# Uneven row groups (65 and 63 rows per partition) in a top-2 dispatch kernel, and one early store less

## The chip, the cores and the metric

The kernel runs on one core of a Trainium2 chip. The metric is the device time of one execution in microseconds; lower is better. The other cores are idle.

## The reference

```python
batch, seq, hidden, n_experts, k = 16, 1024, 512, 8, 2
logits_max = np.max(router_logits, axis=-1, keepdims=True)
probs = np.exp(router_logits - logits_max)
probs = probs / np.sum(probs, axis=-1, keepdims=True)
topk_indices = np.argsort(probs, axis=-1)[..., -k:]
topk_probs = np.take_along_axis(probs, topk_indices, axis=-1)
topk_probs = topk_probs / np.sum(topk_probs, axis=-1, keepdims=True)
x_expanded = x[:, :, np.newaxis, :].repeat(k, axis=2)
return (x_expanded * topk_probs[..., np.newaxis]).astype(np.float32)
```

There are 16384 rows (tokens) of 512 float32 values. For each row, the softmax weights of the two best of eight experts are normalized to a sum of one, the smaller first. The output holds each row of x twice, once times each weight. So 33.6 MB of x and 0.5 MB of logits are read, and 67.1 MB are written: an x row has 2 KiB, an output row (both copies) 4 KiB.

## The kernel before

Row p x 128 + m lies on partition p: each of the 128 partitions owns 128 consecutive rows, m = 0 to 127. In memory two neighbouring partitions therefore stand 128 rows apart, 256 KiB in x and 512 KiB in the output.

`top2_weights` finds the two largest of eight logits by a tree of maxima and minima on VectorE (lines 26 to 36), takes their difference (L39), and makes both weights as sigmoids of it on ScalarE (L41, L42). The result `WA` holds two weights for every row.

The 128 rows of a partition are worked off in two groups of 64. `xs` is a buffer for 64 rows of x on every partition, and `osp` one for 16 rows of output. A group consists of

- the loads into `xs` (L101): 16 rows each in group 0; 2, 2, 4, 8 and then three times 16 rows in group 1 (`LOADS`);
- one multiplication on VectorE for each tile of rows (L105), which writes both products of each row, and a store of that tile (L113).

There is no room for 64 rows of output beside `xs`, so most tiles write their output over rows of `xs` that are done with. The plan of a group: rows 0 to 15 go to `osp`; rows 16 to 31 over rows 0 to 31 of `xs` (`low`); rows 32 to 39 and 40 to 47 to the two halves of `osp`, once the store of rows 0 to 15 has landed; rows 48 to 63 in tiles of 8, 4 and 4 over rows 32 to 63 (`high`).

In group 0 the first tile is split. Two rows are multiplied and stored first, and that store is issued by ScalarE's queue; the other 14 rows follow. Every other transfer is issued by SyncE's queue, in the order of the program: all loads of a group stand before its stores, and the loads of group 1 behind the last store of group 0. A load or a multiplication that overwrites rows waits until the store that reads them has landed; a queue works in order, so what stands behind a waiting instruction waits too.

Of the kernel before, what the change touches and what calls it, by code (L numbers as in the profile page):

```python
# [1 line left out]

# [4 lines left out]

F32 = mybir.dt.float32
ALU = mybir.AluOpType
ACTF = mybir.ActivationFunctionType  # L10
P = 128


def top2_weights(nc, pool, logits, M, E):

    hi, lo, n = None, None, E
    while n > 1:  # L20
        n //= 2
        if hi is None:
            a, b = logits[:, :, 0:n], logits[:, :, n : 2 * n]
            nhi = pool.tile([P, M, n], F32, tag=f"hi{n}")
            nlo = pool.tile([P, M, n], F32, tag=f"lo{n}")
            nc.vector.tensor_tensor(nhi, a, b, op=ALU.max)  # L26
            nc.vector.tensor_tensor(nlo, a, b, op=ALU.min)  # L27
        else:
            a, b = hi[:, :, 0:n], hi[:, :, n : 2 * n]
            nhi = pool.tile([P, M, n], F32, tag=f"hi{n}")  # L30
            nlo = pool.tile([P, M, n], F32, tag=f"lo{n}")
            tmp = pool.tile([P, M, n], F32, tag=f"tmp{n}")
            nc.vector.tensor_tensor(tmp, lo[:, :, 0:n], lo[:, :, n : 2 * n], op=ALU.max)  # L33
            nc.vector.tensor_tensor(nlo, a, b, op=ALU.min)  # L34
            nc.vector.tensor_tensor(nlo, nlo, tmp, op=ALU.max)  # L35
            nc.vector.tensor_tensor(nhi, a, b, op=ALU.max)  # L36
        hi, lo = nhi, nlo
    dlt = pool.tile([P, M], F32, tag="dlt")
    nc.vector.tensor_tensor(dlt, hi[:, :, 0], lo[:, :, 0], op=ALU.subtract)  # L39
    WA = pool.tile([P, M, 2], F32, tag="WA")  # L40
    nc.scalar.activation(WA[:, :, 0], dlt, ACTF.Sigmoid, scale=-1.0)  # L41
    nc.scalar.activation(WA[:, :, 1], dlt, ACTF.Sigmoid, scale=1.0)  # L42
    return WA

LOADS = [[16] * 4, [2, 2, 4, 8] + [16] * 3]


@with_exitstack  # L50
def kernel(
    ctx: ExitStack,
    tc: tile.TileContext,
    x: bass.AP,
    router_logits: bass.AP,
    k: bass.AP,
    out: bass.AP,
):
    nc = tc.nc
    B, S, D = x.shape  # L60
    E = router_logits.shape[-1]
    N = B * S
    assert int(k) == 2 and E == 8 and N % P == 0
    M = N // P

    GROUP = 64
    L = 16
    x_v = x.rearrange("b s d -> (b s) d").rearrange("(p m) d -> p m d", p=P)
    o_v = out.rearrange("b s k d -> (b s) k d").rearrange("(p m) k d -> p m k d", p=P)
    rl_v = router_logits.rearrange("b s e -> (b s) e").rearrange(  # L70
        "(p m) e -> p m e", p=P
    )

    wpool = ctx.enter_context(tc.tile_pool(name="wpool", bufs=1))
    logits = wpool.tile([P, M, E], F32)
    nc.sync.dma_start(logits, rl_v)  # L76
    WA = top2_weights(nc, wpool, logits, M, E)

    xs = wpool.tile([P, GROUP, D], F32)
    osp = wpool.tile([P, L, 2, D], F32)  # L80


    low = xs[:, : 2 * L, :].rearrange("p (r k) d -> p r k d", k=2)
    high = xs[:, 2 * L :, :].rearrange("p (r k) d -> p r k d", k=2)
    h = L // 2
    e = 2
    begin = [[(0, e, osp[:, :e]), (e, L - e, osp[:, e:])], [(0, L, osp)]]
    plan = [
        (L, L, low),
        (2 * L, h, osp[:, :h]),  # L90
        (2 * L + h, h, osp[:, h:]),
        (3 * L, h, high[:, :h]),
        (3 * L + h, h // 2, high[:, h : h + h // 2]),
        (3 * L + h + h // 2, h // 2, high[:, h + h // 2 :]),
    ]

    for g in range(M // GROUP):
        m0 = g * GROUP
        r = 0
        for n in LOADS[g]:  # L100
            nc.sync.dma_start(xs[:, r : r + n, :], x_v[:, m0 + r : m0 + r + n, :])  # L101
            r += n
        for r, n, og in begin[g] + plan:
            rows = slice(m0 + r, m0 + r + n)
            nc.vector.tensor_tensor(  # L105
                og,
                xs[:, r : r + n, :].unsqueeze(2).to_broadcast([P, n, 2, D]),
                WA[:, rows, :].unsqueeze(3).to_broadcast([P, n, 2, D]),
                op=ALU.mult,
            )  # L110

            queue = nc.scalar if rows.start == 0 else nc.sync
            queue.dma_start(o_v[:, rows], og)  # L113


# [1 line left out]
_INS = ['x', 'router_logits', 'k']  # L117
_OUTS = [((16, 1024, 2, 512), 'float32')]

_NUMBERS = {'k': 2}  # L120


# [26 lines left out]
```

## Time and profile before

| | |
|---|---|
| median of 3 runs | 241.12 us (240.81 to 241.35) |
| profiled execution | 240.86 us, span 239.1 us |
| VectorE busy | 142.4 us (60%) |
| ScalarE busy | 1.8 us |
| moved by DMA | 101.19 MB, mean 423 GB/s |
| one 16-row tile on VectorE | about 17.2 us |
| one 8-row tile on VectorE | about 8.7 us |
| loads of 16 rows | 4096 KB each, median 38.0 us from issue to landing |

The span is from the first to the last instruction of the profiled execution. A DMA share of 1.00 means that all 16 DMA engines of the core were busy all the time. A transfer's time from issue to landing includes the time in which it stands behind other transfers in its queue, so it says little about how fast the transfer itself is. The chain of work that ended last is put down to DMA for 44% and to VectorE for 36%; where a transfer is followed back to its issue, that chain names the instruction that released the issue, even when the queue was still full at that moment.

### The profile page before, as it was taken

What the parts mean: (1) busy time and instruction counts of PE and PEld (TensorE: products, weight loads), DVE (VectorE), ACT (ScalarE), POOL (GpSimd) and SP (SyncE); (2) the same over time, 40 slices, a digit from 0 to 9 for tenths busy, and PEclk for the clock granted to TensorE, in tenths of its full rate; (3) what the DMA queues carried; (4) which work ended last, traced back from release to release, by engine and by line L of the source; (5) the groups of instructions that cost most, each with busy time, mean ns of one, the idle gap of its engine ahead of it and who ended that gap; (6) DMA issues with size and microseconds to landing.
All of it is one profiled execution on the core that took longest, in us unless ns stands there. A gap on an engine that the chain in (4) does not pass through costs nothing.

```text
span 239.1 us, 121 instructions
## 1 busy us (share of the span) xinstructions
DVE 142.4 (60%) x26; ACT 1.8 (1%) x3; POOL 0.2 (0%) x4
## 2 busy tenths in 40 slices
DVE  3369999910499999400000999997008999990000
ACT  2000000000000000000000000000000000000000
POOL 0000000000000000000000000000000000000000
DMA  8999999979989899999999999999999998999996
GB/s 329 400 422 384 461 433 428 511 326 451 504 351 526 351 439 439 439 439 395 436 384 452 439 439 439 433 444 471 406 450 428 406 471 362 428 439 439 439 414 288
DMA packets 3888, 101.19 MB, mean 423 GB/s; under 512 B 432, under 2 KB 432, under 8 KB 816
## 3 DMA queue, kind: packets, MB, share of 16 engines
q1 hardware_dynamic: 3744, 100.14, 97.8%
q10 hardware_dynamic: 144, 1.05, 1.0%
HBM read 34.08 MB, written 67.11 MB: 423 GB/s over the span
## 4 chain that ended last, share of the span: by engine, by line
DMA 44%; DVE 36%; issue 7%; SPq 2%; DVEq 0%
DMA out_dram<-osp 26%; DVE osp L105 22%; DMA xs<-in_x_dram 18%; DVE xs L105 15%; SPq L101 1%; SPq L76 0%; SPq L113 0%; DVEq L105 0%
## 5 line engine op out<-in xcount | busy, mean ns | idle before, releaser
L105 DVE TENSOR_TENSOR osp<-xs,WA 128x8192 f32<-128x8192 f32 (+3 forms) x7 | 69.1, 9908 | 68.3 <-DMA xs<-in_x_dram 39.4
L105 DVE TENSOR_TENSOR xs<-xs,WA 128x4096 f32<-128x4096 f32 (+2 forms) x8 | 69.5, 8691 | 0.3
L26 DVE TENSOR_TENSOR nhi<-logits 128x512 f32<-128x512 f32 x1 | 0.7, 693 | 4.1 <-DMA logits<-in_router_logits_dram 4.1
L41 ACT ACT_TABLE_LOAD x1 | 1.3, 1283 | 0.7 <-PEq L130 0.7
L34 DVE TENSOR_TENSOR nlo<-nhi 128x256 f32<-128x256 f32 (+1 forms) x2 | 0.7, 352 | 0.0
L36 DVE TENSOR_TENSOR nhi<-nhi 128x256 f32<-128x256 f32 (+1 forms) x2 | 0.7, 352 | 0.0
L33 DVE TENSOR_TENSOR tmp<-nlo 128x256 f32<-128x256 f32 (+1 forms) x2 | 0.7, 351 | 0.0
L35 DVE TENSOR_TENSOR nlo<-nlo,tmp 128x256 f32<-128x256 f32 (+1 forms) x2 | 0.7, 350 | 0.0
L27 DVE TENSOR_TENSOR nlo<-logits 128x512 f32<-128x512 f32 x1 | 0.7, 686 | 0.0
L41 ACT ACTIVATE WA<-dlt 128x128 f32<-128x128 f32 x1 | 0.3, 316 | 5.9 <-DVE dlt L39 5.9
L39 DVE TENSOR_TENSOR dlt<-nhi,nlo 128x128 f32<-128x128 f32 x1 | 0.3, 291 | 0.0
L42 ACT ACTIVATE WA<-dlt 128x128 f32<-128x128 f32 x1 | 0.3, 297 | 0.0
L130 POOL MEMSET const-bfloat16-1.0<- 128x1 bf16 x1 | 0.1, 102 | 0.0
L130 POOL MEMSET const-uint8-127<- 128x1 uint8 x1 | 0.1, 102 | 0.0
L130 POOL MEMSET const-float32-0.0<- 128x1 f32 x1 | 0.1, 99 | 0.2 <-issue 0.2
L130 POOL MEMSET const-float32-1.0<- 128x1 f32 x1 | 0.1, 99 | 0.0
## 6 DMA issues: line engine op xcount, KB each, us to landing
xs<-in_x_dram SPq DMA_DIRECT2D x7, 4096.0 KB, 38.0
out_dram<-osp SPq DMA_DIRECT2D x4, 4096.0 KB, 20.7
out_dram<-xs SPq DMA_DIRECT2D x2, 4096.0 KB, 22.2
out_dram<-xs SPq DMA_DIRECT2D x4, 2048.0 KB, 22.8
out_dram<-osp SPq DMA_DIRECT2D x1, 7168.0 KB, 31.9
xs<-in_x_dram SPq DMA_DIRECT2D x1, 2048.0 KB, 29.5
out_dram<-osp ACTq DMA_DIRECT2D x1, 1024.0 KB, 16.5
xs<-in_x_dram SPq DMA_DIRECT2D x2, 512.0 KB, 24.4
```

The lines of the kernel that those rows point to most:

```text
L26: nc.vector.tensor_tensor(nhi, a, b, op=ALU.max)
L27: nc.vector.tensor_tensor(nlo, a, b, op=ALU.min)
L33: nc.vector.tensor_tensor(tmp, lo[:, :, 0:n], lo[:, :, n : 2 * n], op=ALU.max)
L34: nc.vector.tensor_tensor(nlo, a, b, op=ALU.min)
L35: nc.vector.tensor_tensor(nlo, nlo, tmp, op=ALU.max)
L36: nc.vector.tensor_tensor(nhi, a, b, op=ALU.max)
L39: nc.vector.tensor_tensor(dlt, hi[:, :, 0], lo[:, :, 0], op=ALU.subtract)
L41: nc.scalar.activation(WA[:, :, 0], dlt, ACTF.Sigmoid, scale=-1.0)
L42: nc.scalar.activation(WA[:, :, 1], dlt, ACTF.Sigmoid, scale=1.0)
L101: nc.sync.dma_start(xs[:, r : r + n, :], x_v[:, m0 + r : m0 + r + n, :])
L105: nc.vector.tensor_tensor(og, xs[:, r : r + n, :].unsqueeze(2).to_broadcast([P, n, 2, D]), WA[:, rows, :].unsqueeze(3).to_broadcast([P, n, ...
L130: nc = _bacc.Bacc("TRN2", target_bir_lowering=False, num_devices=1)
```

## The change

The two groups get 65 and 63 rows per partition, and each group is a contiguous piece of x, of the logits and of the output: group 0 is the first 128 x 65 rows, group 1 the last 128 x 63. Within a group, partition p owns 65 (63) consecutive rows. Neighbouring partitions stand 65 or 63 rows apart, 130 or 126 KiB in x and 260 or 252 KiB in the output.

What follows from it:

- The logits come in two loads, one for each group.
- `xs` has 65 rows. The last load of group 0 has 17 rows, that of group 1 has 15.
- The last three tiles of a group have 8, 4 and 5 (or 3) rows, and lie so that their output ends with the last row of the group: the function `over` gives rows 2r - G onward of `xs` to the tile that begins at row r. In group 0 the tile of rows 48 to 55 goes over rows 31 to 46; in group 1 over rows 33 to 48.
- The first minimum of `top2_weights` is written over its own input in `logits`, which saves a buffer.

The early store of two rows is gone as well: the first tile of group 0 has 16 rows, as in group 1, and all transfers are issued by SyncE's queue.

```diff
-            nlo = pool.tile([P, M, n], F32, tag=f"lo{n}")
+            nlo = b
...
-LOADS = [[16] * 4, [2, 2, 4, 8] + [16] * 3]
+GROUPS = [65, 63]
+
+LOADS = [[16, 16, 16, 17], [2, 2, 4, 8, 16, 16, 15]]
...
-    x_v = x.rearrange("b s d -> (b s) d").rearrange("(p m) d -> p m d", p=P)
...
+    x_v, o_v, rl_v = [], [], []
+    t0 = 0
+    for n in GROUPS:
+        t1 = t0 + P * n
+        x_v.append(
+            x.rearrange("b s d -> (b s) d")[t0:t1].rearrange("(p m) d -> p m d", p=P)
+        )
...
-    nc.sync.dma_start(logits, rl_v)
+    nc.sync.dma_start(logits[:, : GROUPS[0]], rl_v[0])
+    nc.sync.dma_start(logits[:, GROUPS[0] :], rl_v[1])
...
-    xs = wpool.tile([P, GROUP, D], F32)
+    xs = wpool.tile([P, max(GROUPS), D], F32)
...
-    low = xs[:, : 2 * L, :].rearrange("p (r k) d -> p r k d", k=2)
-    high = xs[:, 2 * L :, :].rearrange("p (r k) d -> p r k d", k=2)
+    def over(r, n, G):
+        a = 2 * r - G
+        return xs[:, a : a + 2 * n, :].rearrange("p (r k) d -> p r k d", k=2)
...
-    begin = [[(0, e, osp[:, :e]), (e, L - e, osp[:, e:])], [(0, L, osp)]]
...
-        (3 * L, h, high[:, :h]),
-        (3 * L + h, h // 2, high[:, h : h + h // 2]),
-        (3 * L + h + h // 2, h // 2, high[:, h + h // 2 :]),
...
+        begin = [(0, L, osp)]
+        plan = begin + [
+            (L, L, over(L, L, 2 * L)),
+            (2 * L, h, osp[:, :h]),
+            (2 * L + h, h, osp[:, h:]),
+        ]
+        plan += [(r, n, over(r, n, G)) for r, n in ((48, 8), (56, 4), (60, G - 60))]
...
-            queue = nc.scalar if rows.start == 0 else nc.sync
-            queue.dma_start(o_v[:, rows], og)
+            nc.sync.dma_start(o_v[g][:, r : r + n], og)
```

More of the change, by code (lines that the diff above doesn't have):

```diff
@@ L62 @@
     N = B * S
-    assert int(k) == 2 and E == 8 and N % P == 0
+    assert int(k) == 2 and E == 8 and N == P * sum(GROUPS)
     M = N // P
-    GROUP = 64
     L = 16
-    x_v = x.rearrange("b s d -> (b s) d").rearrange("(p m) d -> p m d", p=P)
[L69 to L72, printed above, removed]
+    x_v, o_v, rl_v = [], [], []
[5 more added lines that the diff above has]
+        )
+        o_v.append(
+            out.rearrange("b s k d -> (b s) k d")[t0:t1].rearrange(
+                "(p m) k d -> p m k d", p=P
+            )
+        )
+        rl_v.append(
+            router_logits.rearrange("b s e -> (b s) e")[t0:t1].rearrange(
+                "(p m) e -> p m e", p=P
+            )
+        )
+        t0 = t1
@@ L84 @@
-    high = xs[:, 2 * L :, :].rearrange("p (r k) d -> p r k d", k=2)
+    def over(r, n, G):
+        a = 2 * r - G
+        return xs[:, a : a + 2 * n, :].rearrange("p (r k) d -> p r k d", k=2)
     h = L // 2
-    e = 2
-    begin = [[(0, e, osp[:, :e]), (e, L - e, osp[:, e:])], [(0, L, osp)]]
[L88 to L91, printed above, removed]
-        (3 * L, h, high[:, :h]),
-        (3 * L + h, h // 2, high[:, h : h + h // 2]),
-        (3 * L + h + h // 2, h // 2, high[:, h + h // 2 :]),
-    ]
@@ L97 @@
-    for g in range(M // GROUP):
-        m0 = g * GROUP
+    m0 = 0
+    for g, G in enumerate(GROUPS):
         r = 0
         for n in LOADS[g]:
-            nc.sync.dma_start(xs[:, r : r + n, :], x_v[:, m0 + r : m0 + r + n, :])
+            nc.sync.dma_start(xs[:, r : r + n, :], x_v[g][:, r : r + n, :])
             r += n
-        for r, n, og in begin[g] + plan:
-            rows = slice(m0 + r, m0 + r + n)
+        assert r == G
+        begin = [(0, L, osp)]
[5 more added lines that the diff above has]
+        plan += [(r, n, over(r, n, G)) for r, n in ((48, 8), (56, 4), (60, G - 60))]
+        for r, n, og in plan:
@@ L107 @@
                 xs[:, r : r + n, :].unsqueeze(2).to_broadcast([P, n, 2, D]),
-                WA[:, rows, :].unsqueeze(3).to_broadcast([P, n, 2, D]),
+                WA[:, m0 + r : m0 + r + n, :].unsqueeze(3).to_broadcast([P, n, 2, D]),
                 op=ALU.mult,
             )
-            queue = nc.scalar if rows.start == 0 else nc.sync
-            queue.dma_start(o_v[:, rows], og)
+            nc.sync.dma_start(o_v[g][:, r : r + n], og)
+        m0 += G
 _INS = ['x', 'router_logits', 'k']
```

## The prediction

> **What bounds the kernel now.** I read the page's busy times first, then the DMA queues, then the chain of waits, and then the DMA share and rate in stretches chosen from the timeline. The page gives the first two:
>
> ```profile
> DVE 142.4 (60%) x26; ACT 1.8 (1%) x3; POOL 0.2 (0%) x4
> DMA  8999999979989899999999999999999998999996
> ...
> DMA packets 3888, 101.19 MB, mean 423 GB/s; under 512 B 432, under 2 KB 432, under 8 KB 816
> ...
> q1 hardware_dynamic: 3744, 100.14, 97.8%
> q10 hardware_dynamic: 144, 1.05, 1.0%
> ```
>
> VectorE works 60% of the span. The two DMA queues together keep the 16 DMA engines at work for 97.8 + 1.0 = 98.8% of it: 236.2 of 239.1 us. The remaining 2.9 us are the two ends: nothing moves before the first descriptors arrive, and the last write has to be confirmed. The other engines' waits, long as they look, therefore cost nothing so long as the queue holds work:
>
> ```profile
> DVE osp L105 <- DMA xs<-in_x_dram: 39.4, 2, 33.4
> DVE osp L105 <- DMA out_dram<-osp: 28.9, 2, 14.8
> ...
> SPq L113 <- DVE osp L105: 116.4, 6, 28.1
> ...
> SPq L101 <- DMA out_dram<-xs: 17.3, 2, 10.3
> ```
>
> These are lines of the waits of the engines and of SyncE's queue (total, times, longest). VectorE waits 68.3 us for transfers; the transfers wait for nobody. So time can come from two things alone: fewer bytes, or bytes moved faster. The bytes are fixed (34.08 MB read, 67.11 MB written). The question is how far the packets are from their best speed. For that I took windows; the columns are the stretch, its length, busy time of VectorE, ScalarE and GpSimd, the TensorE clock, the DMA share and GB/s:
>
> ```profile
> 3.00:18.00 15.00, 7.84 (x13) 0.51 (x2) 0.00 (x0) 1.00 1.03 440
> 18.00:24.00 6.00, 6.00 (x1) 0.00 (x0) 0.00 (x0) 1.00 0.96 366
> 24.00:42.00 18.00, 17.97 (x2) 0.00 (x0) 0.00 (x0) 1.00 1.04 450
> 42.00:120.00 78.00, 41.27 (x6) 0.00 (x0) 0.00 (x0) 1.00 1.00 430
> 120.00:126.00 6.00, 0.00 (x0) 0.00 (x0) 0.00 (x0) 1.00 1.00 396
> 126.00:158.00 32.00, 26.35 (x2) 0.00 (x0) 0.00 (x0) 1.00 1.01 436
> 158.00:236.00 78.00, 42.93 (x6) 0.00 (x0) 0.00 (x0) 1.00 1.00 431
> ```
>
> Large packets are counted at one moment, so a single window's rate wanders; the rate divided by the share does not. It is 440/1.03 = 427, 433, 430, 432 and 431 GB/s for loads (126 to 158 is loads alone) and for stores (42 to 82, 158 to 236) alike. Only two stretches fall below: 18 to 24 us with 366/0.96 = 381, and 120 to 126 with 396. In time: 18 to 24 was busy 0.96 x 6 = 5.76 us and at 430 would need 366 x 6 / 430 = 5.11, so 0.65 us are lost. 120 to 126 loses 6 - 396 x 6 / 430 = 0.47. The whole of the span: 101.19 MB at 430 GB/s are 235.3 us of the 236.2 that the engines were busy. No change that leaves the bytes alone can give much more than 1 us.
>
> **What the Trainium skill says.** "DMA: Bandwidth & Descriptors", section Bandwidth (Where 436 GB/s comes from), puts the ceiling of one core's 16 DMA engines at 435.2 GB/s. The trace's 430 per full share is 99% of it, so the engines and not the memory are the limit here. The same page, section Latency and other measured facts (HBM row pitch at large powers of two), bears directly on the change: copies between HBM tensors at a partition pitch of 512 KiB ran at 207 GB/s per direction, and 214 when a larger pitch was padded by 4 KiB. In the kernel before, output has a pitch of exactly 512 KiB (128 rows of 4 KiB) and x of 256 KiB. The 3% that this would suggest is not in the trace: stores alone run at 430 to 431. Third, its section Queues, rings and completion order says that each DMA engine takes turns between its queues, a packet at a time; the early store is the one transfer on a second queue (q10). The trace shows that such a store lands 16.5 us after its issue, with the loads going on beside it.
>
> **The change, part by part.**
>
> *No early store.* Before, the first two rows (1.05 MB, 2.29 us on VectorE) go out on ScalarE's queue at 16.21 us, and the other 14 rows at 31.21 on SyncE's. Now one operation makes 16 rows: one such of group 1 took 17.23 us, so from 13.89 to 31.1, and one store goes out then. Does the DMA queue run dry without the early one? The four loads hold 16.8 MB and keep the engines until about 41 us, 10 us after the store is issued. So the early store fills no hole. It only puts 1.05 MB ahead that then lies behind: zero in bytes. What it may take away is the slow stretch at 18 to 24 us: this is the only stretch of plain 16-row loads that is slow, it begins 2 us after the early store's issue, and the same loads in group 1 (126 to 158 us, no second queue) run at 432. Bounds: 0 (a coincidence) to -0.65 us. I take -0.65.
>
> *Pitch.* The pitch of x becomes 65 or 63 rows of 2 KiB, that of output the same of 4 KiB. Where the packets already run at 430 nothing can be won. The other slow stretch, 120 to 126 us, holds the turn from stores to the 2-, 2- and 4-row loads of group 1, whose packets are short (4 and 8 KB); these stay. Bounds: -0.47 us (all of that goes) to a loss, which is the rival below. I take 0.
>
> *Logits in two loads.* Rows of 520 and 504 elements, 2080 and 2016 bytes for a partition in place of 4096. One more issue on SyncE ahead of the x loads: 0.4 us (the first took 0.38; four x loads took 1.91). Before, x is issued at 1.16 us but its data come only after the logits on the same queue, which land 3.4 us after their issue, so the issue hides behind that latency. 128 packets more, 8 on each engine. "DMA: Bandwidth & Descriptors", How a descriptor splits into AXI transactions, says that starts off a 256-byte boundary fetch extra beats: 2080 isn't a multiple of 256. An estimate from both: 0.1 us, with bounds 0 and 0.4 (the whole issue). VectorE waits for both (4.1 us now), but its small operations end at 8.2 us and the first x load lands at 13.8, so 5 us hide that, and the in-place minimum (strided output, same 512 elements, 0.69 us).
>
> *Rows 65 and 63.* Group 0 loads and stores one row more (0.61 us of load and 1.22 of store at 430 GB/s), group 1 one less: zero.
>
> *A new wait.* In group 0 the tile of rows 48 to 55 is now written over rows 31 to 46 of xs, and row 31 holds output of the 16-row store issued at 48.47 us, which lands 33.6 us later, at about 82.1. Before, VectorE began this tile at 80.56. With the longer load ahead (+0.6) it starts at about 82.7, 2.1 us later. Behind it on VectorE are the tiles of 4 and now 5 rows (4.42 and, by 1.07 us a row, 5.5), and behind their stores on SyncE the seven loads of group 1. But at 82 us the queue holds two stores of 4.2 MB from osp, 2 x 9.75 = 19.5 us, so until 102; the delayed store is issued at 91.4. Slack: 10 us. The last store is issued at 98.2 + 2.1 + 1.1 = 101.4, with queued work until 102 + 14.6 = 116.6; loads start to be issued right then, before 122.7 when the queue would be empty. The load of rows 16 to 31 now waits for the store from rows 31 to 46 (landing about 112.2) and the last load for the last store (123), when 48 rows of loads, 29 us, are queued. In group 1 the tile goes to rows 33 to 48 and doesn't touch the 16-row store. Cost: 0, hidden behind the DMA queue.
>
> *End.* The last store has 3 rows rather than 4, but VectorE ends at 215 and the queue at about 238; the end is the queue's. 0.
>
> Sum against the profiled span: 239.1 - 0.65 + 0.1 = 238.5. The profiled execution took 240.86, the three runs have a median of 241.12, so I count the difference, -0.55, from the median: 241.12 - 0.55 = 240.57, and take 240.5.
>
> **Rivals.**
>
> 1. *The slow stretch had another cause, or the logits eat the gain.* Against it: the same loads in group 1 show no such stretch. For it: one execution only. Then 241.1.
>
> 2. *The pitch counts too.* All the short excess goes, -0.65 - 0.47 and, at the start (loads in 3 to 18 us at 427 against 430), 0.1: about 239.9; with executions in which slow packets are more frequent than in this one, 239.3. For it: the skill's figures on pitch. Against it: stores at exactly 512 KiB run at full rate.
>
> 3. *Slower: packets that begin at odd multiples of 2 KiB move more slowly.* Before, every 16-row load begins at a multiple of 32 KiB and every 16-row store at one of 64 KiB in its tensor; after, most don't. The trace before shows no such packet. The place is every x and output packet, 236 us of busy time, so a loss of 0.45% (1.05 us) already outweighs the gain and passes the measurable bound. If reads alone ran as in 18 to 24 us (381 against 430), 34 MB cost 10 us more; 1% on everything is 2.4 us: 242.9. Against it: all starts remain multiples of 2 KiB, thus of 256 bytes, so the rule on extra beats asks nothing.
>
> That the pitch does nothing at all, whatever the change says of it, is part of the forecast.
>
> **How the numbers follow.** What a measurement of this kernel can tell from no change is about 0.2%, 0.48 us: faster is below 240.64, slower above 241.60. Chances: the forecast 45% (about two thirds of it below 240.64, as 240.57 and the bounds of the logits show), rival 1 15%, rival 2 22%, rival 3 18%. Faster: 0.31 + 0.22 = 0.53; same: 0.13 + 0.15 (rival 1) = 0.28; slower: 0.01 + 0.18 = 0.19. Range: 239.2, where rival 2 ends, to 242.6, which takes in the smaller third of rival 3; some 0.15 is left out. The forecast's own range is 240.2 to 241.0.
>
> **What the changed profile would show.** Right: q10 gone; rate over share near 430 in 18 to 24 us; VectorE's first 16-row tile ending near 31.1; a wait of some 2 us of VectorE on out_dram<-xs at 80 to 83 us and no dent in the DMA row there; busy share still near 98.8%. Wrong: loads or stores at another rate over share than 430 (rival 3 below it), the slow stretch still there (rival 1), 120 to 126 us at 430 (rival 2), or a hole in the DMA row after 100 us, which would make the new wait the cause.

## The result and the profile after

The changed kernel takes 243.09 us (median of 4 runs, 242.69 to 243.29) where the kernel before takes 240.97 in the same comparison: a ratio of 1.0084, with a 95% interval of 1.0065 to 1.0102. It is 2.1 us slower. The forecast was 240.5, faster by 0.6; the range ended at 242.6.

First the lines of the page that answer to those of before (busy times, DMA row, packets, queue):

```profile
DVE 142.4 (59%) x25; ACT 1.8 (1%) x3; POOL 0.2 (0%) x4
...
DMA  7999999998989899999999999999898989999993
...
DMA packets 3888, 101.19 MB, mean 419 GB/s; under 512 B 432, under 2 KB 560, under 8 KB 944
...
q1 hardware_dynamic: 3888, 101.19, 97.8%
```

The span is 241.5 us. The DMA engines were busy for 97.8% of it, 236.2 us: the busy time of before (98.8% of 239.1). So the packets have not become slower on the whole. The 2.4 us that the span has grown are time in which DMA engines were idle, and the DMA row says where: its first digit fell from 8 to 7, its last from 6 to 3. The windows of the changed kernel (stretch, length, busy time of three engines, clock, DMA share, GB/s) confirm that the middle isn't to blame:

```profile
3.00:18.00 15.00, 5.41 (x12) 0.51 (x2) 0.00 (x0) 1.00 1.02 429
18.00:24.00 6.00, 6.00 (x1) 0.00 (x0) 0.00 (x0) 1.00 1.01 437
...
36.00:44.00 8.00, 8.00 (x1) 0.00 (x0) 0.00 (x0) 1.00 0.99 377
...
42.00:120.00 78.00, 44.80 (x6) 0.00 (x0) 0.00 (x0) 1.00 1.00 430
120.00:126.00 6.00, 0.00 (x0) 0.00 (x0) 0.00 (x0) 1.00 0.96 404
126.00:158.00 32.00, 22.04 (x2) 0.00 (x0) 0.00 (x0) 1.00 1.02 439
158.00:236.00 78.00, 46.18 (x6) 0.00 (x0) 0.00 (x0) 1.00 1.00 431
```

Rate over share is 430 again in the long stretches. The slow stretch at 18 to 24 us is gone (433), as forecast, but a new one stands at 36 to 44: 377/0.99 = 381 GB/s, where the kernel before had 393 at a share of 0.91, which is 432. Where the time went is seen at the two ends. In the timelines, the first tile of before, and then the x loads and the first and the delayed tile of the changed kernel:

```profile
13.89 17.29 DVE L105 TENSOR_TENSOR osp<-xs,WA 128x2048 f32<-128x2048 f32 x2 [5.98 <-DMA xs<-in_x_dram]
```

```profile
1.64 1.86 SPq L112 DMA_DIRECT2D xs<-in_x_dram  x4
...
16.41 17.23 DVE L123 TENSOR_TENSOR osp<-xs,WA 128x16384 f32<-128x16384 f32 x1 [8.21 <-DMA xs<-in_x_dram]
...
86.15 18.68 DVE L123 TENSOR_TENSOR xs<-xs,WA 128x8192 f32<-128x8192 f32 x3 [2.05 <-DMA out_dram<-xs]
```

The x loads are issued 0.48 us later (1.64 instead of 1.16), but the first of them has landed 2.52 us later. And at the end, in windows of the last microseconds, first of before and then of the changed kernel:

```profile
237.00:238.00 1.00, 0.00 (x0) 0.00 (x0) 0.00 (x0) 1.00 0.09 33
238.00:239.00 1.00, 0.00 (x0) 0.00 (x0) 0.00 (x0) 1.00 0.00 0
```

```profile
237.00:238.00 1.00, 0.00 (x0) 0.00 (x0) 0.00 (x0) 1.00 0.21 86
238.00:239.00 1.00, 0.00 (x0) 0.00 (x0) 0.00 (x0) 1.00 0.09 37
239.00:240.00 1.00, 0.00 (x0) 0.00 (x0) 0.00 (x0) 1.00 0.06 25
```

A share of 0.06 is one engine in 16. So after 238 us fourteen or fifteen engines have nothing left and one or two still work. The packet records of the trace tie the two ends together. They don't name the engine, but an x packet takes 1.21 us, so packets that begin within 0.5 us of each other run on different engines. In the kernel before, 16 x packets begin between 3.26 and 3.77 us, the first ones of the 16 engines. In the changed kernel, 14 engines start theirs between 3.53 and 3.89, one at 4.36 and the last at 5.85 us (every packet between these follows the end of an earlier one); these two first packets are slow as well, 1.99 and 1.64 us. The trace also has 16 increments of a semaphore for every landed transfer, as many as there are engines. Those of one transfer lie 0.4 to 0.7 us apart in the kernel before. In the changed kernel they lie 2.5 to 2.6 us apart on the first three x loads and 2.9 to 3.2 from the fourth on. Of the last store to land, 14 increments come by 237.9 us, one at 239.2 and one at 240.5. The lag is as large at the end as at the start, as if each engine had a fixed share of every transfer: an engine that starts late stays late, and the span ends with it.

That gave theory A: the second logits load, put ahead of x, makes some engines late with the x load. Its rival B: the start addresses of the new pitch do.

### The profile page after: what moved, and what is told of

It reads as the page before. It is cut to its first block, busy times and chain, and to the rows that moved or that the text cites. A ratio compares the mean times of both kernels' runs of the same rounds, so it can differ in the third digit from the quotient of the medians.

```text
span 241.5 us, 121 instructions
## 1 busy us (share of the span) xinstructions
DVE 142.4 (59%) x25; ACT 1.8 (1%) x3; POOL 0.2 (0%) x4
## 3 DMA queue, kind: packets, MB, share of 16 engines
q1 hardware_dynamic: 3888, 101.19, 97.8%
## 4 chain that ended last, share of the span: by engine, by line
DMA 45%; DVE 40%; issue 4%; SPq 1%; DVEq 0%
DVE xs L123 22%; DVE osp L123 18%; DMA xs<-in_x_dram 18%; DMA out_dram<-xs 15%; DMA out_dram<-osp 13%; SPq L112 1%; SPq L92 0%; SPq L91 0%; SPq L130 0%; DVEq L123 0%
## 5 line engine op out<-in xcount | busy, mean ns | idle before, releaser
L123 DVE TENSOR_TENSOR osp<-xs,WA 128x8192 f32<-128x8192 f32 (+1 forms) x6 | 69.0, 11534 | 68.7 <-DMA xs<-in_x_dram 39.3
L123 DVE TENSOR_TENSOR xs<-xs,WA 128x16384 f32<-128x16384 f32 (+4 forms) x8 | 69.5, 8692 | 2.3 <-DMA out_dram<-xs 2.1
L28 DVE TENSOR_TENSOR logits<-logits 128x512 f32<-128x512 f32 x1 | 0.7, 691 | 0.0
## 6 DMA issues: line engine op xcount, KB each, us to landing
out_dram<-osp SPq DMA_DIRECT2D x4, 4096.0 KB, 20.7
```

Source lines behind the costliest of these rows:

```text
L123: nc.vector.tensor_tensor(og, xs[:, r : r + n, :].unsqueeze(2).to_broadcast([P, n, 2, D]), WA[:, m0 + r : m0 + r + n, :].unsqueeze(3).to_b ...
```

## The experiments

**The logits, one load or two.** In the first run the changed kernel gets one logits load; in the second the kernel before gets two.

```diff
-    nc.sync.dma_start(logits[:, : GROUPS[0]], rl_v[0])
-    nc.sync.dma_start(logits[:, GROUPS[0] :], rl_v[1])
+    rl_one = router_logits.rearrange("b s e -> (b s) e").rearrange(
+        "(p m) e -> p m e", p=P
+    )
+    nc.sync.dma_start(logits, rl_one)
```

> The changed kernel with the logits in one load of 4096 bytes per partition by the old row order (so the weights belong to other rows; everything else as in the changed kernel). Theory A, the second logits load delays the descriptors of the first x load on two of the 16 DMA engines and the lag of 2.5 us lasts to the end: the first tile starts near 13.9 us rather than 16.4, nothing moves after 238.5, and the time goes back to 240.3 to 241.0. Theory B, the start addresses of the new pitch make two engines late: the first tile still starts near 16.4 and the time stays at 242.7 to 243.3.

Measured: 240.89 us, ratio 0.9997 (0.9988 to 1.0005). First tile, from the timeline, and windows of the end:

```profile
14.12 17.23 DVE L125 TENSOR_TENSOR osp<-xs,WA 128x16384 f32<-128x16384 f32 x1 [5.92 <-DMA xs<-in_x_dram]
```

```profile
237.00:238.00 1.00, 0.00 (x0) 0.00 (x0) 0.00 (x0) 1.00 0.18 74
238.00:239.00 1.00, 0.00 (x0) 0.00 (x0) 0.00 (x0) 1.00 0.00 0
```

The lag is gone, and with it all of the loss, although pitch, groups, the minimum written in place and the missing early store are those of the changed kernel.

```diff
-    nc.sync.dma_start(logits, rl_v)
+    nc.sync.dma_start(logits[:, :65], rl_v[:, :65])
+    nc.sync.dma_start(logits[:, 65:], rl_v[:, 65:])
```

> The kernel before with its logits load cut into 65 and 63 rows (2080 and 2016 bytes per partition, old pitch), nothing else. Theory A: about 2 us slower than before, 242.5 to 243.5, first tile near 16.4 us, one or two engines still moving data after 238.5. Theory B: no change, 240.8 to 241.4, first tile at 13.9 to 14.3.

Measured: 243.74 us, ratio 1.0104 (1.0071 to 1.0136). Its first tile and its end:

```profile
16.79 17.29 DVE L106 TENSOR_TENSOR osp<-xs,WA 128x2048 f32<-128x2048 f32 x2 [8.81 <-DMA xs<-in_x_dram]
```

```profile
238.00:239.00 1.00, 0.00 (x0) 0.00 (x0) 0.00 (x0) 1.00 0.15 66
239.00:240.00 1.00, 0.00 (x0) 0.00 (x0) 0.00 (x0) 1.00 0.08 33
```

The second load alone, at the old pitch, makes the kernel before 2.8 us slower. Theory B falls: the pitch is neither needed nor enough.

**Odd against even.** `GROUPS = [64, 64]` in the changed kernel, with loads of 16 rows throughout.

> The changed kernel with groups of 64 and 64 rows (pitch 128 KiB in x, 256 KiB in the output), logits in two loads of 2048 bytes per partition. Theory A: as slow as the changed kernel, 242.5 to 243.3. Theory A with the odd row length as the cause (2080 is no multiple of 256): 240.3 to 241.0. Theory B, with odd pitch as the cause: 240.3 to 241.0 as well; the one-load run tells these two apart.

Measured: 243.00 us, ratio 1.0079 (1.0054 to 1.0105). Rows of 2048 bytes lag as well as rows of 2080, so the odd row length isn't the cause. The number of late engines differs: in this profile eight engines begin x by 3.8 us and eight between 4.9 and 5.9, and of the last store eight increments come by 238.4 us and the other eight after 239.6.

**What about the second load?** Two runs on the kernel before keep one of its two properties each. In the first, one transfer writes the logits to two places, so every engine gets 16 packets of 2048 bytes (the first maximum and minimum read them from there; those lines are left out below); in the second, two transfers of 64 partitions each bring the same packets as before.

```diff
-    logits = wpool.tile([P, M, E], F32)
-    nc.sync.dma_start(logits, rl_v)
+    logits = wpool.tile([P, 2, 65, E], F32)
+    nc.sync.dma_start(logits[:, :, :64, :], rl_v.rearrange("p (g m) e -> p g m e", g=2))
```

> The kernel before with its one logits load written to two places 65 rows apart in a slightly larger logits tile, so that each DMA engine gets 16 packets of 2048 bytes from one transfer in place of 8 of 4096. If the number of short packets ahead of x makes engines late: as the kernels with two logits loads, 242.5 to 243.8, first tile near 16.4 us. If it is the second transfer: as before, 240.8 to 241.4, first tile at 13.9 to 14.4 us.

Measured: 241.31 us, ratio 1.0018 (1.0009 to 1.0026); first tile at 14.53 us; as in the kernel before, the DMA share of 238 to 239 us is 0.00.

```diff
-    nc.sync.dma_start(logits, rl_v)
+    nc.sync.dma_start(logits[:64], rl_v[:64])
+    nc.sync.dma_start(logits[64:], rl_v[64:])
```

> The kernel before with its logits load cut by partitions, 0 to 63 and 64 to 127: two transfers of 4 packets of 4096 bytes for each engine, the packets as before. If the second transfer makes the x load late on some engines: 242.5 to 243.8. If it is the number of packets: 240.8 to 241.4.

Measured: 243.12 us, ratio 1.0087 (1.0074 to 1.0100); first tile at 16.46 us, and at the end

```profile
238.00:239.00 1.00, 0.00 (x0) 0.00 (x0) 0.00 (x0) 1.00 0.35 147
239.00:240.00 1.00, 0.00 (x0) 0.00 (x0) 0.00 (x0) 1.00 0.15 66
```

some five engines and then two are still at work. It is the second transfer, not the number or the size of the packets (16 short ones cost 0.3 us).

**Longer transfers ahead of x.** The whole logits load twice, at 4096 bytes for a partition each time.

```diff
     nc.sync.dma_start(logits, rl_v)
+    osp = wpool.tile([P, 16, 2, D], F32)
+    nc.sync.dma_start(osp[:, 0, :, :], rl_v.rearrange("p (k m) e -> p k (m e)", k=2))
```

> The kernel before with the whole logits load (4096 bytes per partition) issued twice, the second into a part of osp that is written later; 0.5 MB more are moved, 1.2 us. If the lag is that two short loads end before the descriptors of the third have reached all engines, the longer packets cover it: first tile near 15.1 us, 242.0 to 242.5. If any third transfer is late by a fixed time: first tile near 17.6 us, 244 to 245.

Measured: 242.35 us, ratio 1.0059 (1.0046 to 1.0072), as the theory of cover had it, though the first tile starts 0.5 us later than that expected. The 0.52 MB more account for 1.2 of the 1.4 us. Its first tile:

```profile
15.61 17.29 DVE L106 TENSOR_TENSOR osp<-xs,WA 128x2048 f32<-128x2048 f32 x2 [7.30 <-DMA xs<-in_x_dram]
```

All 16 engines begin x between 4.98 and 5.38 us. So a second transfer ahead of x is not harmful as such. That it does no harm when the two keep the engines at work long enough, and harm when they end early, fits this run and the ones above; no other length was tried.

**Other places for the logits.** First, the changed kernel with its second logits load behind the first x load.

```diff
     nc.sync.dma_start(logits[:, : GROUPS[0]], rl_v[0])
+    nc.sync.dma_start(xs[:, :n, :], x_v[0][:, :n, :])
     nc.sync.dma_start(logits[:, GROUPS[0] :], rl_v[1])
```

> The changed kernel with the second logits load issued behind the first x load rather than ahead of it. The weights come some 10 us later, so the first tile starts near 19 us instead of 16.4; the queue holds loads until 41 us. If the lag comes from the x load standing third behind two short loads: no lag, nothing moves after 238.5 us, 240.6 to 241.2. If the lag comes with the number of loads at the start, wherever they stand: 242.5 to 243.5. If a first tile at 19 us matters by itself: also above 241.5, with a hole in the DMA row near 41 us.

Measured: 240.89 us, ratio 0.9996 (0.9988 to 1.0005). First tile, from the timeline, and the page's DMA row:

```profile
18.53 17.23 DVE L126 TENSOR_TENSOR osp<-xs,WA 128x16384 f32<-128x16384 f32 x1 [0.58 <-ACT WA L43]
```

```profile
DMA  8999999989898999999999999999999989999996
```

The last digit is 6 again. VectorE now starts 2 us later than in the changed kernel, and the kernel is 2.2 us faster: what VectorE loses at the start is hidden behind the loads.

Second, both logits loads on ScalarE's queue (`nc.scalar.dma_start` in both lines).

> The changed kernel with both logits loads issued by ScalarE's queue, x loads alone on SyncE's. If the lag is a matter of the order in one queue, the x load is now first in its queue: no lag, 240.5 to 241.2. If two short loads at the start delay the x load on whatever queue[...]: 242 to 243.5.

Measured: 245.22 us, ratio 1.0175 (1.0161 to 1.0190). Neither expectation held. The timeline and the page's DMA row:

```profile
24.32 0.69 DVE L27 TENSOR_TENSOR nhi<-logits 128x512 f32<-128x512 f32 x1 [24.32 <-DMA logits<-in_router_logits_dram]
...
28.79 17.22 DVE L123 TENSOR_TENSOR osp<-xs,WA 128x16384 f32<-128x16384 f32 x1 [0.58 <-ACT WA L43]
```

```profile
DMA  7999999497979799999999999999999989999996
```

No engine is late here, but the small packets of one queue take turns with x packets of 1.2 us of the other, as the Trainium skill describes ("DMA: Bandwidth & Descriptors", Queues, rings and completion order). In this trace each engine begins one logits packet every 1.29 us, and sixteen turns bring the logits to 24.3 us. The first store is then issued at 46.0, after the loads have run out: the 4 in the DMA row is a hole of 3.3 us with all 16 engines idle. In the run before, VectorE's later start was hidden behind the loads; here it is too late for that, and the DMA engines wait for it.

**The early store.** The kernel before without it.

```diff
-    begin = [[(0, e, osp[:, :e]), (e, L - e, osp[:, e:])], [(0, L, osp)]]
+    begin = [[(0, L, osp)], [(0, L, osp)]]
...
-            queue = nc.scalar if rows.start == 0 else nc.sync
-            queue.dma_start(o_v[:, rows], og)
+            nc.sync.dma_start(o_v[:, rows], og)
```

> The kernel before without the early store alone. The prediction's step: the slow stretch at 18 to 24 us goes and 0.65 us with it, 240.4. The rival, suggested by slow packets at 36 to 43 us in the changed kernel: the first store of the program slows the loads beside it wherever it stands, so the stretch moves to about 36 to 43 us and the time stays within 0.2 us of before.

Measured: 241.36 us, ratio 1.0011 (1.0002 to 1.0020): not faster, but slower, by 0.4 us in the medians and 0.3 by the ratio. The interval, 0.05 to 0.5 us, takes in the 0.2 that the rival allowed. Its windows:

```profile
18.00:24.00 6.00, 6.00 (x1) 0.00 (x0) 0.00 (x0) 1.00 1.00 431
...
36.00:44.00 8.00, 8.00 (x1) 0.00 (x0) 0.00 (x0) 1.00 1.18 451
```

The slow stretch has moved with the first store. At 36 to 44 us it costs 1.18 x 8 - 451 x 8 / 430 = 1.05 us, where it had cost 0.65 at 18 to 24. That difference is of the size measured, but this profile doesn't prove it: its first tile starts at 14.42 us, 0.53 later than in the kernel before, although the edit changes nothing ahead of it.

The packet records show what is slow: x packets, mostly ahead of the store's own. Here those that begin from 39.7 us on take up to 2.13 us instead of 1.21, and the first store packet begins at 43.3. In the kernel before, those from 17.9 to 23.2 us take up to 1.65, and the early store's first packet begins at 20.7. What slows them isn't shown.

Then the early store put back into the kernel with the late logits:

```diff
-        begin = [(0, L, osp)]
+        e = 2
+        begin = [(0, L, osp)] if g else [(0, e, osp[:, :e]), (e, L - e, osp[:, e:])]
...
-            nc.sync.dma_start(o_v[g][:, r : r + n], og)
+            queue = nc.scalar if m0 + r == 0 else nc.sync
+            queue.dma_start(o_v[g][:, r : r + n], og)
```

> The run before it in this group with the early store of two rows put back on ScalarE's queue (issued near 21 us). If the early store gives nothing, as predicted: the same as without, within 0.2 us. From the kernel before without its early store (0.4 us slower): 0.2 to 0.5 us faster than without, 240.2 to 240.8, the fastest of all.

Measured: 240.72 us, ratio 0.9991 (0.9982 to 0.9999), against 0.9996 without. The sign agrees, but the intervals overlap. This version beats the changed kernel, and the one before by 0.1%, at the edge of the interval. Its profile has two slow stretches: 18 to 32 us loses 0.24 us beside the early store, and 44 to 52 us another 1.03 x 8 - 414 x 8 / 430 = 0.54, on the last x packets ahead of the second store (1.6 to 2.1 us where 1.29 is usual for their 34 KB). The kernel with the late logits alone loses 0.95 x 8 - 348 x 8 / 430 = 1.13 at 36 to 44. So an early store takes over a part of the cost, and not always the whole.

**Odd pitch once more,** now without the lag: the same version with `GROUPS = [64, 64]`.

> The changed kernel with the second logits load behind the first x load and the early store put back, and groups of 64 and 64 rows rather than 65 and 63. If odd pitches are worth something by themselves, this is slower than the same kernel with 65 and 63 (240.72 measured), by up to 0.5 us: 241.0 to 241.3. If they aren't: within 0.2 us of 240.72.

Measured: 240.65 us, ratio 0.9985 (0.9969 to 1.0000). Odd pitches give nothing measurable beyond even ones of nearly the same size. One of its 14 executions took 242.97 us, and the other 13 lie between 240.50 and 240.81. The profile is of the one with 242.97; windows of its end:

```profile
237.00:238.00 1.00, 0.00 (x0) 0.00 (x0) 0.00 (x0) 1.00 0.08 33
238.00:239.00 1.00, 0.00 (x0) 0.00 (x0) 0.00 (x0) 1.00 0.04 16
239.00:240.00 1.00, 0.00 (x0) 0.00 (x0) 0.00 (x0) 1.00 0.04 16
```

One engine works alone at the end. Its first x packet began at 4.01 us (15 engines: 2.47 to 3.09) and took 2.04. So in one execution of 14 such a lag came without a second load ahead of x, and it cost about the same, 2.3 us. In the kernels with two short loads every execution is as slow: 242.69 us or more in all 16.

## Why the prediction was wrong

*What bounds the kernel* held: the DMA engines' busy time is 236.2 us in both profiles. But the sentence "So time can come from two things alone: fewer bytes, or bytes moved faster" left out the third: an engine's start. The 2.9 us of the two ends were taken as fixed. They are set by the latest of 16 engines, and a mean share hardly shows that one. "Busy share still near 98.8%" is the sign of being right that failed for this reason (97.8%), and VectorE's first tile ended at 33.6 us, not near 31.1.

*Logits in two loads* is the step that failed. It was put at 0.1 us with bounds 0 and 0.4, the whole issue. It cost 2.2: 243.09 with two loads, 240.89 with one. The bound from above counted the time on SyncE's queue and the beats of the packets, and assumed that the x load's data follow the logits without a gap. On 14 engines they did; on two they came 0.5 and 2 us late. The small operations on VectorE were hidden as supposed; what failed is the start of the x load itself.

*No early store*, put at -0.65, is wrong too. The stretch at 18 to 24 us was the early store's, as supposed: it went with it. But it doesn't need the second queue: without the early store, x packets ahead of SyncE's first store are slow, at 36 to 44 us. In the changed kernel this costs 0.99 x 8 - 377 x 8 / 430 = 0.91 us. The early store itself was worth 0.2 us (late logits) to 0.3 or 0.4 us (kernel before), rather than costing 0.65.

*Pitch*, taken as 0, was nearly right. The stretch of 120 to 126 us lost 0.47 us before and loses 0.96 x 6 - 404 x 6 / 430 = 0.12 after. The run with one logits load loses 0.17 there and the kernel before without its early store 0.46; they differ in the grouping and what comes with it, and in time by 0.5 us in the medians and 0.3 by the ratios (0.9997 and 1.0011, intervals that just overlap). The other profiles agree: this stretch loses 0.16 to 0.66 us in all six of the old layout and 0.12 to 0.17 in six of the grouped one, even groups included; the seventh, with the logits on ScalarE's queue, loses 0.79. So the grouped layout seems to win some 0.3 us. Its odd part wins nothing that was measured. Rival 3, slow packets at odd starts, had the right sign and the wrong place: the stores and loads run at 430. That its example of 242.9 us lies close to the 243.09 measured is luck.

*The new wait* behaved as worked out: 2.05 us on VectorE before the tile of rows 48 to 55, and no dent in the DMA row. *Rows 65 and 63* and the *end's* three rows cost nothing that shows.

The sum of what was measured, +2.2 for the logits, about +0.2 to +0.4 for the early store, about -0.3 for the layout, is +2.1 to +2.3, against +2.1. Only the first of these stands far clear of the noise.

What stays open is why the third transfer reaches some engines late when two short ones stand ahead of it. The issue of x at 1.64 us alone doesn't explain it: with the logits loaded twice x was issued at 1.63, and all engines had its packets by 5.38 us, earlier than the 5.85 of the late engine here. Which engines are late, and what holds them, no run here tells.

## What to carry to other kernels

In a kernel bound by DMA, look at the slowest of the 16 engines and not only at their mean share: in these runs a tail in which the share fell to 1/16 or 2/16 was a lag that an engine had picked up on the first large load and never gave back. Try not to put two short loads ahead of the first large one; here one short load ahead, and a second one behind the large one, cost nothing measurable while the consumer had slack. A slow stretch beside an event is not yet a saving: ask whether the cost will come with the next event of its kind, once this one is gone.

## What the runs showed of the hardware

- Two short transfers (0.5 MB in all) ahead of a large load on one queue cost 2.0 to 2.8 us in four kernels (the changed one and three variants), whatever their row length (2016 to 4096 bytes for a partition); two of 0.5 MB each caused no lag (0.2 us beyond the time of their bytes); one transfer of 16 short packets for each engine costs 0.3 us.
- Nothing evens out an engine's late start: a spread of 2.6 us on the first x load was 3.2 us at the end, 225 us later.
- Loads just ahead of the first store are slow: about 381 GB/s instead of 430 in the profiles of the kernel before, of the changed one and of the kernel before without its early store, 0.65 to 1.05 us in all (0.46 with even groups, 1.13 with the late logits). With an early store and late logits, loads ahead of the second store are slow too (0.24 and 0.54 us).
- A pitch of 512 KiB in the output didn't slow the stores: 430 to 431 GB/s per full share, as at 252 and 260 KiB.
